# TensorE's instructions in the written order, in a hybrid mixer block on one Trainium2 core

## Chip, core and metric

The program runs on one core of a Trainium2 chip (trn2). What is compared is the device time of one execution in microseconds (us). Five engines work in parallel, each with an instruction stream of its own: TensorE (PE in the profile, its weight loads PEld), VectorE (DVE), ScalarE (ACT), GpSimd (POOL) and SyncE (SP, which here issues all DMAs). They wait for each other by semaphores.

## What is computed

One layer of a streaming encoder over 1024 tokens of 1024 channels. u is the RMS-normalised input; it is multiplied by one wide input matrix, and the product is split over four branches of 256 channels:

```python
u = rms_norm(h, norm_mix_pre[l])
z = u @ w_in[l]
(hq, hf, hi, hg, pz, sq, sk, sv, iq, ik, iw, mq) = jnp.split(z, split_pts, axis=-1)
y_a = hgrn2_mixer(hq, hf, hi, hg, lb_all[l], hgrn_norm[l])   # gated linear recurrence, 4 heads
y_b = pool_mixer(pz, pool_w[l], pool_scale[l])               # trailing means over 2, 4, 8, 16 tokens
y_c = dsa_mixer(sq, sk, sv, iq, ik, iw)                      # index scores, top 256 keys, attention
mk, mv = jnp.split(rms_norm(mem, norm_mem[l]) @ w_mem_kv[l], 2, axis=-1)
y_m = mem_attention(mq, mk, mv)                              # attention into 256 memory tokens
merged = None
for bi, y in enumerate((y_a, y_b, y_c, y_m)):
    term = jax.nn.sigmoid(u @ w_gate[l, bi]) * (y @ w_branch[l, bi])
    merged = term if merged is None else merged + term
h = h + rms_norm(merged @ w_out[l], norm_mix_post[l])
gt, up = jnp.split(rms_norm(h, norm_ffn_pre[l]) @ w_ffn_gate_up[l], 2, axis=-1)
h = h + rms_norm((jax.nn.silu(gt) * up) @ w_ffn_down[l], norm_ffn_post[l])
```

## The kernel before

The tokens are worked in two halves of 512 (`HT`), and the second half begins while the first one's FFN is still running. A float32 product is made of three products of the rounded type fp32r: every operand is split into a high and a low part (`split_ps`, `Unit.split`), and hi x hi, hi x lo and lo x hi are added up in a PSUM bank.

Two kinds of work make up the program. The dense stream is a list, `prog`, of units (`Unit`): the weights of a unit (128 x 1024 values) are loaded into `raw` by SP, split into `wh` by ScalarE (L265) and into `wl` by GpSimd or VectorE (L266), and multiplied by 24 matmuls. `raw`, `wh` and `wl` have three buffers each, so that a unit's split waits for the products of the unit three before it. A product is either channel-major (`fm_mm`, L284 to L286, 512 columns, two PSUM banks "B") or token-major (`tm_units`, L341 to L343, four banks "A" or two "B" and two "C"). The other kind is side work: index scores, top-k, the sparse attention (dsa), the memory attention, the HGRN recurrence, pooling, and the normalisation of u. Each of these is a Python generator that emits a few instructions for all engines and yields. The loop over the list sets the written order:

```python
advance(i - e.hold)
e.mm(e)
step_side()
if e.evac is not None:
    e.evac(e)
```

So one step of every running generator is written between a unit's products and the evacuation of its bank; `need(...)` writes all that is left of a generator at once. Side work takes its PSUM bank from the class that `side_tag` names at the time (`spt`).

The kernel is written for a tile framework whose scheduler takes this program, goes through it by priority (the earlier written, the higher) with a model of the engines, and decides for each engine the order of its instructions: where the next one of an engine isn't ready in that model, a later one that is goes ahead. It then sets the semaphores. On the chip each engine follows its fixed order.

Steps that the prediction speaks of, in written order:

- The start: `mem_front` loads the memory tokens and x and squares x; `uT_gen0` has then three kinds of steps: `rstd_cols` (L438, four matmuls with a vector of ones over `xsq`), `to_rows` (L443, the 1 / rms of each token as rows in PSUM), and the pairs of u tiles (L486, L155, L489). One step is written behind each of the four memory units (`kv_units`). Then come the unit `mq[0]`, `kv_out` (`mem_rstd` with L438 and L443 once more, then mk and mv with the transposes L464), the unit `mq[1]`, four units hg (`thg`), with `rows1` (L443) behind the second.
- The first half's middle: four units iq with the index scores behind them (`score_gen`, L596 and L597, relu on ScalarE, accumulation on VectorE), two units pz, four units hi (`thi`), two units sq. `pool_gen` makes the trailing means on VectorE (L952 to L972), splits them into `phl`, and multiplies by L978 to L980: for the first group behind the second hi unit, for the second group behind the third. HGRN of head 0 has L905 behind the first sq unit and L915, L916 behind the second.
- The second half's scores, four tiles with up to 1024 keys, are written behind its units iq and hi.
- `wout_units(1)` ends with tiles that come one after another; `u2_gen` transposes each normalised tile `un` (L203). The last step of it is written by `all_of(S["u2", 1])`, ahead of the FFN's first two units, which `by_token_halves` writes as four products of 24 matmuls over 256 tokens each, the first tokens of both units first.

Of the kernel before, what the change touches and what calls it, by code (L numbers as in the profile page):

```python
# [35 lines left out]
def tile_hybrid_block(ctx, tc, x, x_t, mem_t, cols, w_in, w_gate, w_branch, w_out, hgrn_norm,  # L36
# [3 lines left out]
    x, out = x[0], out[0]  # L40
# [22 lines left out]

    # ---------------------------------------------------------------- constants
    ident = st([128, 128], name="ident")
# [8 lines left out]
    def build_masks():  # L74
        """Inside a block of 32 steps: where s lies in the left and t in the right half of a block of 2^(l+1)."""
        for l in range(6):
            if l < 5:
                m = st([128, 128], name="mtmp", tag="t2")
                h = 1 << l
                nb = 64 // h  # L80
                nc.gpsimd.memset(m, 1.0)
                v = m.rearrange("p (n w) -> p n w", w=2 * h)
                nc.gpsimd.affine_select(out=v, in_=v, pattern=[[-2 * h, nb], [0, 2 * h]], compare_op=OP.is_ge,
                                        fill=0.0, base=0, channel_multiplier=1)
                nc.gpsimd.affine_select(out=v, in_=v, pattern=[[2 * h, nb], [0, 2 * h]], compare_op=OP.is_ge,
                                        fill=0.0, base=h - 1, channel_multiplier=-1)
                nc.gpsimd.memset(v[:, :, 0:h], 0.0)
            else:
                m = ident
            for r in range(4):  # L90
                rs = slice(32 * r, 32 * r + 32)
                nc.vector.tensor_copy(masks[rs, l, :], m[rs, rs])
# [23 lines left out]
    def load_small():  # L116
        dma(hgain, bcast_row(hgrn_norm, 256))
        # lower bound: cumsum over depth of softmax over depth, minus its first row
        lg = st([128, 8], name="lg")
        nc.vector.tensor_tensor(lg[:, 4:8], lb_in, lb_in, op=OP.subtract)  # L120
        nc.scalar.activation(lg[:, 0:4], lg[:, 4:8], AF.Exp)
        rc = st([128, 4], name="lrc")
        nc.vector.reciprocal(rc, lg[:, 0:4])
        nc.vector.tensor_tensor(lg[:, 4:8], lg[:, 0:4], rc, op=OP.mult)
        nc.vector.tensor_tensor(lbt[:, :, 0], lg[:, 4:8], lg[:, 4:8], op=OP.subtract)
        nc.vector.tensor_scalar(lbt[:, :, 1], lbt[:, :, 0], -1.0, 1.0, op0=OP.mult, op1=OP.add)
        pw = st([128, 256], name="pw", tag="t2")
        nc.gpsimd.memset(pw, 0.0)
        for g in range(4):
            r0 = 64 * (g % 2)  # L130
            c0 = (g // 2) * 128 + r0
            dma(pw[r0:r0 + 64, c0:c0 + 64], pool_w[0, g])
        hi = poolw[:, 0].rearrange("p a b -> p (a b)")
        lo = poolw[:, 1].rearrange("p a b -> p (a b)")
        nc.scalar.activation(hi, pw, AF.Copy)
        nc.gpsimd.tensor_tensor(lo, pw, f32(hi), op=OP.subtract)

    # ---------------------------------------------------------------- persistent data
    h1d = [dr.tile([128, D], F32, name=f"h1d{i}", tag=f"h1d{i}") for i in range(8)]
# [12 lines left out]

    # ---------------------------------------------------------------- small helpers
    def copy(o, i):
# [6 lines left out]
    def twice_silu(o, t, p):  # L161
        """2 p sigmoid(p), as p (1 + tanh(p / 2))."""
        nc.scalar.activation(t, p, AF.Tanh, scale=0.5)  # L163
        nc.vector.scalar_tensor_tensor(o, t, 1.0, p, op0=OP.add, op1=OP.mult)  # L164
# [11 lines left out]
    def mean_eps(ss):  # L176
        """Its part of mean + eps, of half of the columns."""
        ms = st([128, 1], name="mse", bufs=10)
        nc.vector.tensor_scalar(ms, ss, 1.0 / D, EPS, op0=OP.mult, op1=OP.add)
        return ms  # L180
# [24 lines left out]

    # ---------------------------------------------------------------- side work
    side = []
# [22 lines left out]

    # ---------------------------------------------------------------- main stream
    class Unit:
        """One step of the dense stream: weights of up to 1024 columns per partition, and a product."""

# [64 lines left out]
    def by_token_halves(u0, u1, x_of):  # L299
        """Two units as four products over half of the tokens each: the first tokens of both come first."""  # L300
        ev0, ev1 = u0.evac, u1.evac

        def mm0(u):
            u.p = pt("B")

        def mm1(u):
            u.p = pt("B")
            for n0 in (0, 256):
                for v in (u0, u1):
                    fm_mm(v, v.p, *x_of(), n0 + 256, n0=n0)  # L310

        u0.mm, u1.mm, u1.hold = mm0, mm1, 1
        u0.evac, u1.evac = None, lambda u: [ev0(u0), ev1(u1)]

    def tm_units(w, ktiles, k0, cols, xT_of, tags, evac, pre=None, defer=0, apart=0):
        """Token-major product: four token tiles accumulate over the k tiles, two per unit.
        The last `defer` units run tile by tile, so that the tiles end one after another;
        the first `apart` of them keep their weights outside of the ring."""
        acc, res, waiting = [], [], []
        n = sum(wd for _, wd in cols)  # L320
        nu = ktiles // 2
        for ui in range(nu):
# [29 lines left out]
            u = Unit(loads, (2, n), mm, end if ui == nu - 1 and not defer else None, pre=pre if ui == 0 else None)  # L352
# [38 lines left out]

    # ================================================================ memory tokens
    S = {}

    def mem_front(load):
        """Memory tokens with their gain; 1 / rms comes in after the product."""
        mh, ml = S["memT"] = (st([128, NK, 256], F32R, name="memh", tag="b8"),
# [35 lines left out]
    def rstd_cols(acc, tag):  # L433
        """1 / rms of every token, a column per token tile, out of the partial sums of squares."""
        n = acc.shape[-1] // 128
        p = pt(tag)
        for t in range(n):
            nc.tensor.matmul(p[:, t:t + 1], acc[:, t * 128:(t + 1) * 128], ones[:, 0:1], start=True, stop=True)  # L438
        return rstd_of(p[:, 0:n], D, n)
# [27 lines left out]

    # ================================================================ u of one half
    def load_x(i):
# [38 lines left out]
    def rows1():  # L508
        """1 / rms of the second half's tokens."""
        rs = st([128, 4], name="xrs")  # L510
        for t in range(4):
            xt = load_x(4 + t)
            r = rstd_of(square_sum(xt, xt), D)
            nc.vector.tensor_copy(rs[:, t:t + 1], r[:, 0:1])
        yield
        copy(rrow, to_rows(rs, 4, spt()))
# [9 lines left out]

    # ================================================================ DSA
    def ikd_alloc(h):
# [18 lines left out]
    def stack_evac(p):  # L547
        """Two heads of 64 channels as [hi; lo] and [lo; hi] over the partitions."""
        q = st([128, 2, HT], F32R, name="qst", tag="b4")
        lo = st([128, HT], F32R, name="qlo", tag="t2")  # L550
# [140 lines left out]

    # ================================================================ memory attention
    def ev_mq(h, c):
# [54 lines left out]

    # ================================================================ HGRN
    def ev_hg(h):  # L750
# [60 lines left out]
    def hgrn_gen(h, hd, fa, fb):  # L811
# [5 lines left out]
        for c in range(4):  # L817
            s = slice(c * 128, (c + 1) * 128)
# [4 lines left out]
        def levels(ls):  # L823
            """Both factors of the decayed products over the halves of every block of 2^(l+1) steps."""
            def views(i, l):
# [18 lines left out]
        def gram32(todo):  # L844
            """Products inside the blocks of 32 steps, of up to four levels in one bank."""
            p = spt()
# [19 lines left out]
        p = spt()  # L866
# [67 lines left out]

    # ================================================================ pooling
    def ev_pz(h, c):
# [48 lines left out]

    # ================================================================ gates, as 2 sigmoid(p) = 1 + tanh(p / 2)
    def gate_units(h, br, ykey, fs, first=False, last=False, pre=None):
# [29 lines left out]

    # ================================================================ output projection
    def stag(tag):
# [45 lines left out]

    # ================================================================ FFN
    def ffn_units(h, groups, late):
# [73 lines left out]

    # ================================================================ program
    def all_of(gen):
# [109 lines left out]
    prog += [lambda: all_of(S["u2", 1])] + ffn_units(1, (8, 8, 6), lambda: None)  # L1253
    run()

# [31 lines left out]
```

## Time and profile before

| | |
|---|---|
| median of 2 runs | 1835.7 us (1834.63 to 1836.76) |
| span of the profiled execution, first to last instruction | 1831.4 us |
| TensorE busy | 1758.4 us, 96% |
| VectorE busy | 1054.4 us, 58% |
| ScalarE busy | 722.3 us, 39% |
| GpSimd busy | 880.5 us, 48% |
| DMA queue of the kernel's loads, share of the 16 engines | 34.0% |
| mean granted TensorE clock | 0.986 |

The profile is that of one execution. Its span lies 4.3 us under the median of the runs, which have some time around the span. The times in the rows count from the span's start. An engine's idle time ahead of an instruction stands in brackets with the instruction that released it. Matmuls overlap in the records: the distance from one start to the next, not the duration of one, is what a product costs in a dense stretch. A product of two operands of plain float32 shows as two records.

### The profile page before, as it was taken

To read this page: it belongs to the slowest core of one execution; us is meant where nothing else is said; L and a number is where in the kernel's file an instruction comes from. 1 tells how busy PE (TensorE), PEld (TensorE's weight loads), DVE (VectorE), ACT (ScalarE), POOL (GpSimd) and SP (SyncE) were. 2 spreads that over 40 slices of the span, in tenths; PEclk is the share of its full clock that TensorE was granted. 3 is DMA by queue.
4 is the path that set the end of the run, shared out by engine and by line. 5 is a ranking of instruction groups with operands and counts; after the bars stand their busy time and mean duration, and the time that the engine had idled before them with its cause. 6 is when DMAs were issued, how large, how long until landed. Compare 5 with 4: busy or idle time off the path is not lost. (4 is left out here: it accounts for less than half of the span.)

```text
span 1831.4 us, 25977 instructions
## 1 busy us (share of the span) xinstructions
PE 1758.4 (96%) x10000; PEld 1462.8 (80%) x10000; DVE 1054.4 (58%) x1972; ACT 722.3 (39%) x1175; POOL 880.5 (48%) x567
## 2 busy tenths in 40 slices
PE   7988989999999999999999999989999999999998
PEld 6877778888887787878888877878878888888886
DVE  6577999482345999999982674567541411011114
ACT  5653435443435533333323454534433422322232
POOL 5533435566643244444444353346566555455453
PEclk9998999999999999999999999999999999999999
DMA  6523222343244232323222442223323543333332
GB/s 180 174 59 86 76 73 74 90 140 117 86 135 120 75 104 82 108 78 94 82 81 90 159 155 73 67 87 84 96 73 92 166 150 100 96 95 101 92 103 70
DMA packets 262300, 185.99 MB, mean 102 GB/s; under 512 B 15904, under 2 KB 234144, under 8 KB 262048
## 3 DMA queue, kind: packets, MB, share of 16 engines
q1 hardware_dynamic: 262176, 184.33, 34.0%
q8 instruction: 79, 1.29, 0.3%
q14 instruction: 45, 0.37, 0.1%
HBM read 169.62 MB, written 10.49 MB: 98 GB/s over the span
## 5 line engine op out<-in xcount | busy, mean ns | idle before, releaser
L266 POOL TENSOR_TENSOR wl<-raw,wh 128x1024 fp32r<-128x1024 f32 (+3 forms) x269 | 636.5, 2367 | 804.6 <-ACT wh L265 770.3
L265 ACT ACTIVATE wh<-raw 128x1024 fp32r<-128x1024 f32 (+4 forms) x274 | 278.3, 1018 | 659.0 <-issue 273.5
L284 PE MATMUL psB<-uTh,wh 128*128 128x512 f32 x816 | 327.2, 401 | 3.1 <-DVE hw L164 2.5
L285 PE MATMUL psB<-uTl,wh 128*128 128x512 f32 x816 | 321.4, 394 | 0.5 <-DVE uTl L489 0.3
L286 PE MATMUL psB<-uTh,wl 128*128 128x512 f32 x816 | 321.7, 394 | 0.0
L284 PE MATMUL psB<-u2h,wh 128*128 128x512 f32 (+1 forms) x720 | 278.4, 387 | 1.4 <-DVE qlo L554 0.9
L285 PE MATMUL psB<-u2l,wh 128*128 128x512 f32 (+1 forms) x720 | 277.2, 385 | 1.2 <-DVE u2l L159 1.2
L286 PE MATMUL psB<-u2h,wl 128*128 128x512 f32 (+1 forms) x720 | 276.8, 385 | 0.0
L284 PEld LDWEIGHTS psB<-uTh,wh 128*128 128x128 f32 x816 | 155.2, 190 | 35.9 <-DVE hw L164 2.9
L286 PEld LDWEIGHTS psB<-uTh,wl 128*128 128x128 f32 x816 | 154.9, 190 | 33.5
L285 PEld LDWEIGHTS psB<-uTl,wh 128*128 128x128 f32 x816 | 155.3, 190 | 32.5 <-DVE uTl L489 1.2
L619 DVE MAX8 m<-sc 128x8 f32<-128x384 f32 (+5 forms) x192 | 170.7, 891 | 3.7
L620 DVE MATCH_REPLACE8 sc<-m,sc 128x384 f32<-128x384 f32 (+5 forms) x192 | 168.0, 875 | 0.1
L284 PEld LDWEIGHTS psB<-u2h,wh 128*128 128x128 f32 x720 | 135.2, 188 | 28.3 <-PE psB L286 1.3
L285 PEld LDWEIGHTS psB<-u2l,wh 128*128 128x128 f32 x720 | 135.3, 188 | 27.8 <-DVE u2l L159 1.4
L286 PEld LDWEIGHTS psB<-u2h,wl 128*128 128x128 f32 x720 | 135.2, 188 | 27.2
L164 DVE SCALAR_TENSOR_TENSOR silu<-silu,psB 128x512 f32<-128x512 f32 x44 | 30.1, 683 | 203.5 <-ACT silu L163 203.4
L1085 DVE SCALAR_TENSOR_TENSOR silu<-silu,psB 128x512 f32<-128x512 f32 x44 | 30.1, 683 | 87.1 <-PE psB L286 87.1
L1003 DVE SCALAR_TENSOR_TENSOR sig<-sig,psC 128x512 f32<-128x512 f32 x48 | 32.9, 685 | 78.6 <-PE psC L286 70.3
L1006 POOL TENSOR_TENSOR merged<-merged,sig 128x512 f32<-128x512 f32 x48 | 64.5, 1345 | 16.1 <-DVE sig L1003 12.7
L341 PE MATMUL psA<-wh,hTh 128*128 128x512 f32 x176 | 69.2, 393 | 0.0
L342 PE MATMUL psA<-wl,hTh 128*128 128x512 f32 x176 | 68.6, 390 | 0.0
(383 smaller groups left out, 3060.2 us busy)
## 6 DMA issues: line engine op xcount, KB each, us to landing
raw<-in_w_ffn_gate_up_dram SPq DMA_DIRECT2D x88, 512.0 KB, 3.9
raw<-in_w_gate_dram SPq DMA_DIRECT2D x64, 512.0 KB, 3.9
raw<-in_w_ffn_down_dram SPq DMA_DIRECT2D x44, 512.0 KB, 3.7
raw<-in_w_in_dram SPq DMA_DIRECT2D x36, 512.0 KB, 4.1
praw<-in_w_branch_dram SPq DMA_DIRECT2D x64, 128.0 KB, 3.5
raw<-in_w_out_dram SPq DMA_DIRECT2D x16, 512.0 KB, 3.8
xt<-in_x_t_dram SPq DMA_DIRECT2D x12, 512.0 KB, 6.0
xt<-in_x_dram SPq DMA_DIRECT2D x12, 512.0 KB, 4.9
```

The source lines that it names most:

```text
L164: nc.vector.scalar_tensor_tensor(o, t, 1.0, p, op0=OP.add, op1=OP.mult)
L265: nc.scalar.activation(self.hi[:, r], self.raw[:, r], AF.Copy)
L266: eng.tensor_tensor(self.lo[:, r], self.raw[:, r], f32(self.hi[:, r]), op=OP.subtract)
L284: nc.tensor.matmul(p[:, ns], whi[:, k, :], xh[:, k, ns], start=(k == 0), stop=False)
L285: nc.tensor.matmul(p[:, ns], whi[:, k, :], xl[:, k, ns], start=False, stop=False)
L286: nc.tensor.matmul(p[:, ns], wlo[:, k, :], xh[:, k, ns], start=False, stop=(k == nk - 1))
L341: nc.tensor.matmul(acc[t][:, 0:n], xh[:, k, ts_], v.hi[:, a, :], start=(k == 0), stop=False)
L342: nc.tensor.matmul(acc[t][:, 0:n], xh[:, k, ts_], v.lo[:, a, :], start=False, stop=False)
L619: nc.vector.max(m8, sc)
L620: nc.vector.match_replace(sc, m8, sc, DROPPED)
L1003: nc.vector.scalar_tensor_tensor(o, sg, 1.0, u.q, op0=OP.add, op1=OP.mult)
L1006: nc.gpsimd.tensor_tensor(m, m, sg, op=OP.add)
```

## The change

The loop over the list is run inside a block that tells the scheduler to leave the order of TensorE as it is written. The scheduler still orders VectorE, ScalarE, GpSimd and SP by its model. No instruction is added, removed or altered; comments and docstrings are dropped without a change of the line numbers.

```diff
     prog += wout_units(1)
     prog += [lambda: all_of(S["u2", 1])] + ffn_units(1, (8, 8, 6), lambda: None)
-    run()
+    with tc.manual_schedule(engines={mybir.EngineType.PE}):
+        run()
```

## Rows read from the trace of the kernel before

**Rows 1.** The page's head and busy time: engine, busy us, share, instructions; clock by slice; a costly group.

```profile
span 1831.4 us, 25977 instructions
...
PE 1758.4 (96%) x10000; PEld 1462.8 (80%) x10000; DVE 1054.4 (58%) x1972; ACT 722.3 (39%) x1175; POOL 880.5 (48%) x567
...
PEclk9998999999999999999999999999999999999999
...
L266 POOL TENSOR_TENSOR wl<-raw,wh 128x1024 fp32r<-128x1024 f32 (+3 forms) x269 | 636.5, 2367 | 804.6 <-ACT wh L265 770.3
```

**Rows 2.** Sums by stretch: busy us and instructions by engine, granted clock, DMA share.

```profile
150.05:153.55 3.50, 3.50 (x25) 3.46 (x25) 3.43 (x7) 1.09 (x3) 1.58 (x1) 1.00 0.11 23
...
153.60:187.70 34.10, 25.63 (x113) 22.40 (x112) 29.24 (x65) 9.06 (x15) 10.12 (x4) 0.80 0.26 75
...
161.20:167.20 6.00, 5.99 (x21) 5.70 (x22) 4.58 (x10) 2.19 (x4) 2.42 (x1) 0.50 0.22 63
...
187.70:300.00 112.30, 104.32 (x710) 86.74 (x709) 107.16 (x280) 53.45 (x90) 45.98 (x29) 0.97 0.27 76
...
1080.10:1086.10 6.00, 6.00 (x26) 4.96 (x27) 2.77 (x2) 3.51 (x5) 5.76 (x3) 1.00 0.30 87
...
1480.00:1800.00 320.00, 320.00 (x1414) 264.96 (x1413) 34.38 (x50) 87.96 (x109) 167.62 (x80) 1.00 0.32 97
```

**Rows 3.** TensorE's timeline, the first 46 us: start, us, instruction, idle before.

```profile
6.34 0.58 PE L284 MATMUL psA<-memh,wh 128*128 128x256 f32 x1 [6.34 <-ACT wh L265]
...
12.57 0.41 PE L284 MATMUL psA<-memh,wh 128*128 128x256 f32 x1
...
23.47 1.50 PE L438 MATMUL psC<-ones,xsq 128*128 128x1 f32 x8 [2.26 <-DVE xsq L498]
...
26.74 2.08 PE L443 MATMUL psC<-ident,rstd 128*128 128x128 f32 x8 [0.93 <-POOL rstd L168]
...
45.83 0.38 PE L464 MATMUL psC<-ident,mvT 128*128 128x128 f32 x2
...
45.96 0.37 PE L341 MATMUL psA<-wh,uTh 128*128 128x264 f32 x1
```

**Rows 4.** VectorE's and GpSimd's timelines, the same stretch.

```profile
22.72 0.69 DVE L498 TENSOR_TENSOR xsq<-xsq 128x512 f32<-128x512 f32 x1
...
39.41 0.14 DVE L173 TENSOR_SCALAR ms<-psC 128x2 f32<-128x2 f32 x1
...
40.31 1.28 POOL L489 TENSOR_TENSOR uTl<-xt,uTh 128x512 fp32r<-128x512 f32 x1
```

**Rows 5.** TensorE's timeline, 157 to 188 us.

```profile
157.12 0.31 PE L341 MATMUL psA<-wh,uTh 128*128 128x320 f32 x1
...
161.21 0.79 PE L978 MATMUL psC<-phl,poolw 128*128 128x512 f32 x1 [3.78 <-ACT phl L155]
...
179.78 1.94 PE L905 MATMUL psA<-vg,hw 128*128 128x64 f32 x8 [4.69 <-DVE svt L772]
...
187.66 0.33 PE L915 MATMUL psA<-vg,att 128*128 128x64 f32 x2
```

**Rows 6.** VectorE's timeline at 180 us.

```profile
180.26 0.68 DVE L975 TENSOR_TENSOR phl<-pz,phl 128x512 fp32r<-128x512 f32 x1
```

**Rows 7.** TensorE's timeline, 1459 to 1467 us.

```profile
1459.11 0.48 PE L284 MATMUL psB<-u2h,wh 128*128 128x256 f32 x2
...
1466.44 1.07 PE L203 MATMUL psA<-ident,un 128*128 128x128 f32 x8 [0.68 <-DVE un L195]
```

**Rows 8.** TensorE's timeline at four single places.

```profile
242.80 0.65 PE L870 MATMUL psA<-hw 128*32 128x32 f32 x16 [5.59 <-DVE yc L159]
...
612.34 0.50 PE L596 MATMUL psC<-ikd,qst 128*128 128x512 f32 x1 [1.30 <-ACT relu L599]
...
1080.09 0.50 PE L284 MATMUL psB<-uTh,wh 128*128 128x512 f32 x1 [2.51 <-DVE hw L164]
...
1359.32 0.63 PE L931 MATMUL psA<-ident,hw 128*128 128x128 f32 x4 [1.03 <-DVE hw L924]
```
## Prediction

> **What bounds the kernel now.** Read the page first: TensorE is busy 1758.4 of 1831.4 us and holds its full clock in nearly every slice [rows 1]. From 1480 to 1800 us it has no idle time at all: 1414 products in 320 us, one each 0.226 us [rows 2]. So a microsecond in which TensorE stands idle is a microsecond of the kernel, unless it takes the place of one that TensorE stands already. Second, go through TensorE's timeline from start to end with the code beside it. The written order is: a unit's products, then one step of every side generator, then the unit's evacuation. Where an instruction of a side step stands behind products that the code has after it, the scheduler has moved it, and the count of those products is what the change will take out of that hole. Third, look at what ended the idle time ahead of the moved instruction: where the row names a releaser, its input really came late, and in the written order TensorE would have waited for it with nothing to do.
>
> The result of that reading: at most places of the 1831 us the order is already the written one. I find it changed at the start (up to 73 us), around the pooling branch of the first half (153 to 188), in the index scores of the second half (580 to 634), at the last token tile before the last FFN (1459), and at eight smaller places with 4 to 20 products each.
>
> **The start.** Today the scheduler runs all of the four memory products nearly back to back. In the code, step 1 of the generator of u (L438, the sums of squares) stands behind the first of them, the rows (L443) behind the second. The first one's 24 products run from 6.34 to 12.57, and xsq is ready at 22.72 + 0.69 = 23.41 [rows 3, 4]. In the written order TensorE stands from 12.6 to 23.4; L438 starts when it does today, but the other 72 memory products are still to come. The second 24 take 5 us at the low clock that follows a long wait (the first 24 took 6.2), so L443 starts near 30.0, not at 26.74: u is 3.3 us late. Today u's last part is ready at 40.31 + 1.28 = 41.6 [rows 4]; then 44.9, and the first mq unit ends at 45.3. Behind it the code has kv_out, a chain through VectorE, GpSimd, ScalarE and back (ms, rstd, L443, mk, mvT, L464). Today that took from 39.41 to 45.83 beside the products of the second mq unit [rows 3, 4]; then nothing is beside it: 6 us, and after it that unit, 24 x 0.226 = 5.4. That is 56.7 where today it is 45.96: 10.7 us late. The clock may fall once more during kv_out (3 us), and the rows of the second half (L443 in rows1) may come late for their written place (up to 5). I take 13, between 10 and 19.
>
> **Pooling, first half.** The matmuls of the first pooling group (L978) stand behind the second of the four hi units, those of the second group behind the third. Today 25 products of later units run first, at 0.14 us each (25 in 3.5) [rows 2], and TensorE still waits 3.78 for phl, until 161.21; the second group's wait is hidden behind a whole hi unit, a whole sq unit and six more products, until its phl is ready at 180.26 + 0.68 = 180.9 [rows 5, 6]. VectorE sets both times: busy 29.24 of the 34.1 us, most of it top-k and pooling in turn [rows 2]. Written order: wait from 153.6 to 161.2; the group until 163.9; the third hi unit, partly at the low clock, until 169; wait until 180; the group until 182; the fourth hi unit at the low clock, 6.4; two sq units of 5.5 and L905 with about 1.5. That is 200.9 for L915, today at 187.66 [rows 5]: 13 us. VectorE has less to give way to when TensorE, and so GpSimd's weight splits, stand still; I take 11, between 7 and 14.
>
> **The last token tile.** all_of(u2) puts the transposes of the fourth tile ahead of the whole FFN. Its un is ready at 1466.4; today 40 products of the first two FFN units run from 1459.11 on, ahead of it [rows 7]. Written order: TensorE stands 7.3 us. The 40 products have 256 columns; at half of 0.226 they are worth 4.5, and the hole less the 0.68 that is idle today is 6.6. After such a wait the clock is low, about 3 us more. I take 8, between 4.5 and 9.
>
> **The scores, 580 to 634.** A step emits up to eight pairs of L596 and L597 through two psC buffers; each needs ScalarE's relu and VectorE's accumulation to free the next. Today 40 products in all lie between the pairs, and in three of the blocks TensorE waits over a microsecond beside, as at 612.34 [rows 8]. Worth at most 27 x 0.14 + 13 x 0.226 = 6.7; the pairs can come a little sooner when nothing stands between them. I take 5, between 1 and 7.
>
> **The smaller places.** An upper end is the moved products by 0.226: 10 at the second half's pooling (2.3) and 12 at L931 (2.7); 4, 6, 7, 5 and some 20 short ones at the others (in all 5). I take 9, between 5 and 13; the 13 has one more fall of the clock, at L931, whose wait grows from 1.03 to 4 [rows 8].
>
> **What comes back.** VectorE is the busiest engine from 187.7 to 300: 107.16 of 112.3 us [rows 2], and TensorE is idle for 8.0 there (104.32 busy), 5.59 of it at 242.80, for VectorE [rows 8]. It isn't idle while TensorE stands between 153 and 188: top-k goes on and ends sooner. I take 4 back, between 0 and 9.
>
> **The weights.** Nothing else is moved: the instructions of TensorE issue no DMA. But a unit's split waits for the products three units before it (wh has three buffers), and SP's load of raw waits for the split, so ScalarE, GpSimd and SP stand still too when TensorE does. Their cover is three units, some 16 us, and starts again with TensorE; I cost this at nothing, and a unit whose weights come late after a long wait would cost some 2.4, GpSimd's part of its split [rows 1].
>
> **The clock.** Six microseconds after the 3.78 us wait all ran at 0.50 of full speed, 1.2 GHz; after the 2.51 us wait at 1080 the clock stayed at 1.00 [rows 2, 8]. So I charge a fall to long waits alone: 3 us each, half of six. The Trainium skill speaks against this change here: "TensorE: Matmul & The Clock Gate", section "HAM oscillation — how this bites in real kernels", tells that waits between groups of matmuls put the array back to half clock, so that each group starts cold and pays again. The first row agrees, the second is a wait that it didn't follow. By the page the new waits at kv_out, L931 and in the scores would each cost a fall, and the sum would be some 10 us higher; that is a rival below.
>
> **The sum.** 13 + 11 + 8 + 5 + 9 - 4 = 42. The profiled execution's span is 1831.4 us, and the median of the runs is 1835.7, so 4.3 lie around the span. 1831.4 + 42 + 4.3 = 1877.7; I say 1878 us, 2.3% slower. From the ends of all parts: 1835.7 + 18.5 = 1854 and 1835.7 + 62 = 1898.
>
> **Rivals.** (1) VectorE gets ahead, and the kernel is not measurably slower. Place: 153 to 300 us. Each microsecond that TensorE stands goes to a saturated VectorE, so the second phl comes 4 us sooner, and the 8.0 us of waits up to 300 go with the fall of the clock behind the longest (3). It decides when top-k is over before the scores of its last tile are used. Price: 42 less 4, less the 7 not yet counted, less 4 where the score pairs flow freely: 27, so 1863. For it: VectorE is the only engine near 100% there. Against it: it does its work in a fixed order, and top-k instructions stand between those for which TensorE waits.
> (2) The clock falls after every new wait: three more falls, 10 us, 1888. For it the row at 161, against it the one at 1080.
> (3) The other engines are ordered anew around a TensorE that stands still: top-k instructions go in front of evacuations, and from 640 to 900, where VectorE is as full as it is from 187.7 on, TensorE waits at places where it doesn't now. One more wait like 5.59 in each of the five dsa tiles or so is 28 us: 1905. Against it: where the order is the written one already, the scheduler has no reason to do so.
> (4) The change does nothing, because order and waits stay as they are: 1836. Against it: the timeline shows orders that the code doesn't have.
>
> **How the numbers follow.** Chances: the forecast 0.38, with 1866 to 1890 as its own range; rival 1 0.27; rival 2 0.18; rival 3 0.11; rival 4 0.06. Two per cent, about what a measurement can tell from no change, end at 1872.4. Three quarters of the forecast (0.29) and rivals 2 and 3 lie above: 0.58. The rest of the forecast, rivals 1 and 4 within: 0.40. Faster needs the waits of today to go and no new ones to come: 0.02. The range of 8 in 10 goes from 1856, below rival 1, to 1900, between rivals 2 and 3.
>
> **What would show it.** In the new profile: no product of a memory unit between 12.6 and 23.4; the clock low after that; L978 at 161 and about 180 (plus the 13 of the start) with waits of 7 and 11 us ahead of them; a wait of 7 us ahead of L203 before the last FFN; TensorE's idle time up by some 35 us with the same 10000 instructions. The wait at 242.80 tells rival 1 from the forecast, the clock behind kv_out and L931 rival 2, waits between 640 and 900 rival 3. I am wrong if the late inputs come sooner once TensorE stands for them, above all xsq and phl.

## The result and the profile after

The changed kernel takes 1882.8 us in the median (1881.27 to 1884.27), 1.026 times the kernel before, with an interval of 1.023 to 1.029: 2.6% slower. The forecast was 1878, between 1856 and 1900. Two executions among those of the experiments below, of 6810.5 and 2000.2 us, ran at a low granted clock (0.461 and 0.827) and are in none of the times.

The page of the changed kernel answers to [rows 1]: span, busy time by engine, granted clock by slice.

```profile
span 1879.5 us, 25981 instructions
...
PE 1767.8 (94%) x10000; PEld 1471.0 (78%) x10000; DVE 1049.2 (56%) x1972; ACT 726.2 (39%) x1177; POOL 877.1 (47%) x567
...
PEclk8898999999999999999999999999999999999999
```

The same 10000 instructions of TensorE. Idle time is span less busy time: 1831.4 - 1758.4 = 73.0 before, 1879.5 - 1767.8 = 111.7 after, so 38.7 more. The other 9.4 of the 48.1 is busy time: the same products at a lower clock (the mean granted clock is 0.974, before 0.986).

TensorE waits for these in the changed kernel (what waited, what it waited for, us in total, times, longest us). Ahead of the same instructions the kernel before waits 2.26 (L438), 3.78 (the first L978 alone), and 0.68 (L203) [rows 3, 5, 7].

```profile
PE psC L978 <- ACT phl L155: 14.7, 2, 7.4
PE psC L438 <- DVE xsq L498: 10.7, 1, 10.7
PE psC L596 <- ACT relu L599: 8.0, 11, 1.3
PE psA L203 <- DVE un L195: 7.8, 2, 7.0
```

TensorE's timeline at the start, against [rows 3]:

```profile
7.43 0.58 PE L284 MATMUL psA<-memh,wh 128*128 128x256 f32 x1 [7.43 <-ACT wh L265]
...
13.39 0.41 PE L286 MATMUL psA<-memh,wl 128*128 128x256 f32 x1
...
24.54 1.84 PE L438 MATMUL psC<-ones,xsq 128*128 128x1 f32 x8 [10.73 <-DVE xsq L498]
...
49.10 1.22 PE L443 MATMUL psC<-ident,rstd 128*128 128x128 f32 x4 [1.04 <-POOL rstd L168]
52.92 1.09 PE L464 MATMUL psC<-ident,mvT 128*128 128x128 f32 x4 [2.60 <-DVE mvT L461]
53.66 0.78 PE L284 MATMUL psB<-uTh,wh 128*128 128x512 f32 x1
...
61.43 0.28 PE L341 MATMUL psA<-wh,uTh 128*128 128x264 f32 x1
...
73.42 1.65 PE L443 MATMUL psC<-ident,xrs 128*128 128x128 f32 x6 [4.74 <-ACT P L725]
```

VectorE's timeline says why L438 and L464 start when they do, against [rows 4]:

```profile
23.70 0.69 DVE L498 TENSOR_TENSOR xsq<-xsq 128x512 f32<-128x512 f32 x1
...
52.36 0.75 DVE L461 TENSOR_TENSOR mvT<-psA,mrstd 128x256 f32<-128x256 f32 x2
```

No product stands between 13.8 and 24.5; xsq, which needs nothing from TensorE, ends at 24.39, one us later than before, as the first product of this execution does. What is lost is the 72 products that stood in front of L438 before. The second mq unit starts behind L464, and L341 comes 15.5 us later than before (45.96).

TensorE's timeline at the first half's pooling, against [rows 5, 6]:

```profile
182.29 0.79 PE L978 MATMUL psC<-phl,poolw 128*128 128x512 f32 x1 [7.37 <-ACT phl L155]
...
197.12 0.80 PE L978 MATMUL psC<-phl,poolw 128*128 128x512 f32 x1 [7.29 <-ACT phl L155]
...
209.42 1.00 PE L905 MATMUL psA<-vg,hw 128*128 128x64 f32 x8
...
215.80 0.33 PE L915 MATMUL psA<-vg,att 128*128 128x64 f32 x2
```

At four other places, against [rows 7, 8]:

```profile
267.10 0.43 PE L870 MATMUL psA<-hw 128*32 128x32 f32 x8 [4.56 <-DVE yc L159]
...
642.94 0.79 PE L596 MATMUL psC<-ikd,qst 128*128 128x512 f32 x1 [1.28 <-ACT relu L599]
...
1396.19 0.86 PE L931 MATMUL psA<-ident,hw 128*128 128x128 f32 x4 [3.83 <-DVE hw L924]
...
1507.57 1.73 PE L203 MATMUL psA<-ident,un 128*128 128x128 f32 x7 [7.04 <-DVE un L195]
```

And sums by stretch (columns as in [rows 2]), of the changed kernel:

```profile
182.24:197.07 14.83, 7.12 (x27) 6.16 (x27) 14.22 (x33) 2.32 (x3) 2.34 (x1) 0.73 0.12 35
...
208.80:324.70 115.90, 110.78 (x745) 92.61 (x744) 108.86 (x280) 55.83 (x93) 48.25 (x30) 0.99 0.30 83
...
597.65:706.50 108.85, 97.87 (x429) 77.37 (x428) 86.95 (x144) 50.18 (x94) 27.98 (x14) 0.94 0.27 76
...
1396.20:1399.60 3.40, 3.40 (x11) 2.81 (x12) 0.69 (x1) 0.60 (x1) 0.00 (x0) 0.53 0.00 0
...
1507.50:1512.50 5.00, 4.93 (x23) 4.96 (x24) 1.38 (x2) 1.19 (x2) 0.00 (x0) 0.50 0.98 341
```

and two of the kernel before, the time from the end of the first phl's high part (for which L978 waits) to that of the second's, as in the first line above, and the same 429 instructions at the scores:

```profile
161.16:180.05 18.89, 14.15 (x58) 12.36 (x58) 17.11 (x33) 5.65 (x10) 7.70 (x3) 0.77 0.28 82
...
569.30:666.70 97.40, 91.52 (x429) 74.41 (x428) 81.75 (x133) 49.97 (x94) 28.05 (x14) 0.98 0.31 84
```

The second phl's high part ends there at 180.04:

```profile
179.41 0.63 ACT L155 ACTIVATE phl<-pz 128x512 fp32r<-128x512 f32 x1 [4.75 <-DVE pz L972]
```

Read the two lines of the scores (597.65 to 706.50 and 569.30 to 666.70) together: 11.5 us more, of which 10.98 - 5.88 = 5.1 is idle time and 97.87 - 91.52 = 6.35 is busy time, with the clock at 0.94 against 0.98. The waits of about 1 us at L596 cost less than the low clock among them.

**Where the 48 us arise.** The dense stream has 6912 products in every kernel here (L284 to L286, L341 to L343; where the start is mended, 24 of them stand in a function of their own), in one order but for some products near a moved step. The table takes the n-th of them, says when it starts in the kernel before, and how much later the n-th starts in the others, in us of their profiled executions. The columns behind "whole" belong to the experiments below.

| n, before | whole | start | first half | scores | rest | start mended | pooling | tail | banks | all | all, free | pooling, free |
|---|---|---|---|---|---|---|---|---|---|---|---|---|
| 144, 46.0 | 15.5 | 13.8 | -0.8 | 0.4 | 0.4 | 3.8 | 14.4 | 14.1 | 13.6 | 4.7 | -0.9 | -0.5 |
| 312, 92.9 | 21.8 | 21.9 | -0.8 | 0.5 | 0.7 | 12.3 | 20.6 | 20.3 | 19.9 | 10.1 | -4.0 | -0.4 |
| 400, 124.6 | 21.1 | 21.8 | 2.9 | 0.5 | -0.9 | 13.1 | 19.9 | 19.6 | 19.2 | 16.4 | 0.6 | -0.6 |
| 700, 213.8 | 28.2 | 21.6 | 10.7 | 0.5 | -0.9 | 20.1 | 20.1 | 26.8 | 26.3 | 16.2 | -2.7 | -1.8 |
| 850, 266.8 | 24.7 | 22.1 | 7.3 | 1.6 | 0.6 | 18.2 | 19.2 | 23.3 | 22.8 | 13.2 | -3.3 | -1.9 |
| 2050, 569.3 | 28.4 | 22.1 | 10.2 | 2.4 | 1.3 | 21.5 | 23.2 | 27.3 | 26.5 | 17.1 | -2.6 | -1.8 |
| 2350, 666.7 | 39.8 | 20.6 | 8.7 | 13.0 | -0.1 | 32.0 | 32.2 | 38.1 | 32.4 | 20.5 | -4.4 | -3.2 |
| 3100, 864.3 | 37.4 | 22.1 | 10.2 | 10.5 | -0.2 | 29.5 | 29.7 | 35.6 | 31.6 | 18.3 | -3.3 | -1.6 |
| 4150, 1163.1 | 35.8 | 22.4 | 10.3 | 10.1 | -0.2 | 29.5 | 29.7 | 34.0 | 32.3 | 17.1 | -4.5 | -1.5 |
| 4450, 1250.0 | 36.9 | 22.5 | 10.4 | 10.1 | 1.1 | 31.3 | 22.9 | 35.4 | 34.1 | 10.4 | -11.2 | -8.2 |
| 4900, 1368.9 | 41.2 | 22.6 | 12.7 | 12.3 | 5.4 | 36.1 | 28.6 | 39.6 | 38.9 | 16.0 | -11.0 | -8.0 |
| 5350, 1471.1 | 48.0 | 22.5 | 12.6 | 12.3 | 12.3 | 43.0 | 34.4 | 40.3 | 45.9 | 16.7 | -11.0 | -8.0 |

### The profile page after: what moved, and what is told of

Same layout as the page of the kernel before. It is cut to its first block, busy times and chain, and to the rows that moved or that the text cites. A ratio compares the mean times of both kernels' runs of the same rounds, so it can differ in the third digit from the quotient of the medians.

```text
span 1879.5 us, 25981 instructions
## 1 busy us (share of the span) xinstructions
PE 1767.8 (94%) x10000; PEld 1471.0 (78%) x10000; DVE 1049.2 (56%) x1972; ACT 726.2 (39%) x1177; POOL 877.1 (47%) x567
## 5 line engine op out<-in xcount | busy, mean ns | idle before, releaser
L284 PE MATMUL psB<-uTh,wh 128*128 128x512 f32 x816 | 328.7, 403 | 3.6 <-DVE hw L164 2.5
L286 PE MATMUL psB<-uTh,wl 128*128 128x512 f32 x816 | 322.0, 395 | 0.0
L284 PE MATMUL psB<-u2h,wh 128*128 128x512 f32 (+1 forms) x720 | 279.4, 388 | 1.3 <-DVE qlo L554 0.8
L286 PE MATMUL psB<-u2h,wl 128*128 128x512 f32 (+1 forms) x720 | 277.6, 386 | 0.0
L284 PEld LDWEIGHTS psB<-uTh,wh 128*128 128x128 f32 x816 | 156.3, 191 | 37.0 <-DVE hw L164 2.9
L286 PEld LDWEIGHTS psB<-uTh,wl 128*128 128x128 f32 x816 | 155.6, 191 | 33.9
L284 PEld LDWEIGHTS psB<-u2h,wh 128*128 128x128 f32 x720 | 136.1, 189 | 28.3 <-PE psB L286 1.2
L286 PEld LDWEIGHTS psB<-u2h,wl 128*128 128x128 f32 x720 | 135.9, 189 | 27.3
L1006 POOL TENSOR_TENSOR merged<-merged,sig 128x512 f32<-128x512 f32 x48 | 64.7, 1347 | 11.7 <-DVE sig L1003 7.9
L341 PE MATMUL psA<-wh,hTh 128*128 128x512 f32 x176 | 69.3, 394 | 0.0
L343 PE MATMUL psA<-wh,hTl 128*128 128x512 f32 x176 | 68.6, 390 | 0.0
```

Source lines behind the costliest of these rows:

```text
L284: nc.tensor.matmul(p[:, ns], whi[:, k, :], xh[:, k, ns], start=(k == 0), stop=False)
L286: nc.tensor.matmul(p[:, ns], wlo[:, k, :], xh[:, k, ns], start=False, stop=(k == nk - 1))
L341: nc.tensor.matmul(acc[t][:, 0:n], xh[:, k, ts_], v.hi[:, a, :], start=(k == 0), stop=False)
L343: nc.tensor.matmul(acc[t][:, 0:n], xl[:, k, ts_], v.hi[:, a, :], start=False, stop=e)
L1006: nc.gpsimd.tensor_tensor(m, m, sg, op=OP.add)
```

## The experiments

Times of all, each with the kernel before on the same chip:

| kernel | median us | before | ratio (95%) |
|---|---|---|---|
| written order at the start alone | 1854.6 | 1832.3 | 1.012 (1.008 to 1.016) |
| in the first half alone | 1843.1 | 1832.3 | 1.006 (1.004 to 1.008) |
| at the second half's scores alone | 1843.9; 1844.1 | 1832.3; 1834.6 | 1.007 (1.004 to 1.009); 1.005 (1.002 to 1.007) |
| in the rest alone | 1846.2 | 1832.3 | 1.008 (1.005 to 1.010) |
| whole, start mended | 1875.8 | 1833.0 | 1.023 (1.022 to 1.025) |
| whole, pooling mended | 1868.7 | 1833.0 | 1.019 (1.018 to 1.021) |
| whole, last tile mended | 1876.2 | 1833.0 | 1.023 (1.022 to 1.025) |
| whole, four banks at the scores | 1880.2 | 1833.0 | 1.026 (1.025 to 1.028) |
| whole, all mended | 1850.7 | 1831.8 | 1.010 (1.008 to 1.011) |
| all mended, scheduler orders TensorE | 1820.6 | 1831.8 | 0.994 (0.992 to 0.995) |
| pooling mended, scheduler orders TensorE | 1826.8 | 1831.8 | 0.997 (0.996 to 0.998) |

**The written order in one stretch at a time.** Theory 1: each place costs its own waits, and the places add up. Theory 2: the other engines, ordered anew, make them depend on each other. Two functions enter and leave the block and stand in the list of units:

```diff
+    def on():
+        held.append(tc.manual_schedule(engines={mybir.EngineType.PE}))
+        held[-1].__enter__()
+
+    def off():
+        held.pop().__exit__(None, None, None)
...
-    with tc.manual_schedule(engines={mybir.EngineType.PE}):
-        run()
+    run()
...
-    prog += [front1] + thg(1)
+    prog += [on, front1] + thg(1)
```

The start, up to skik:

> TensorE keeps the written order only from the first memory unit to the unit skik of the first half (up to 120 us); behind that the scheduler orders it as before. Theory 1 (each place costs its own waits, and the places add up): the 20.7 us that the changed kernel is later at the last hg product than the kernel before, so about 1835.7 + 20.7 = 1856, with waits of 10.7 ahead of the first L438, 2.6 ahead of L464 and 4.7 ahead of L443 of rows1. Theory 2 (the places depend on each other, since the other engines are ordered anew through the whole program, or the late start is given back where VectorE is the bound, 187 to 300 us): clearly less than 20 or more than 25, and the sum of the four kernels of this group is not the 47 of the whole change.

Measured 22.3 us in the medians, 21.9 at product 312 and the same up to the end: the start's cost arises there and nothing of it is given back later, not even from 187 to 300 us, where VectorE is the bound.

The first half:

> TensorE keeps the written order only from head(0, 0) to the first half's last gate unit (120 to 540 us), the pooling of the first half among it. Theory 1: the changed kernel is 6 to 7 us later at the end of this stretch than at its start (5.3 of it at pooling, 2.9 at L631, 2 given back at L870), so about 1842; waits of 7 us ahead of both L978. Theory 2: when TensorE isn't late already, VectorE is no further ahead, and pooling costs the 11 that was forecast, so 1847 or more.

10.8 us in the medians. The waits ahead of the two L978 are 7.37 and 7.29, the same as in the whole to a hundredth, and pooling costs 7.8 (products 400 to 700) against 7.1, so a late start gives VectorE no lead there; theory 2's reason falls. The time is nearer to 1842 than to 1847. What is beyond theory 1 is 3.7 between 93 and 125 us, which the whole doesn't have, and 2.3 from a wait at L870 (below).

The scores:

> TensorE keeps the written order only from thg(1) to the two sq units of the second half (540 to 680 us): u2's transposes and the index scores with their two psC buffers. Theory 1: 12.3 us, the part of the changed kernel in that stretch (11.5 at the scores), so about 1848; three falls of the clock between 600 and 680. Theory 2 (the scores are only dear because the rest runs in the written order too): the 5 that was forecast, so about 1841.

11.6 us in the medians. To see the places, the same kernel ran once more, with a sharper question:

> The kernel with the written order only from thg(1) to the two sq units of the second half once more, for a profile at the usual clock. Theory 1 (TensorE's stand at the scores lets VectorE get ahead with top-k, and some of it is given back at the attention tiles of 745 to 865 us): 11 to 12 us later than the kernel before at the last sq product, 2 to 2.5 given back until 865, and at the end 9 to 10, so about 1842. Theory 2 (the 2.5 that the changed kernel gives back there comes from its late start): 11 to 12 at both points and at the end, about 1844.

Its line for the scores, and one of its waits:

```profile
571.65:679.70 108.05, 97.34 (x429) 77.09 (x428) 87.03 (x144) 50.22 (x94) 27.98 (x14) 0.95 0.27 76
```

```profile
PE psA L870 <- DVE hw L841: 2.9, 1, 2.9
```

The scores cost 13.0 - 2.4 = 10.6 with no other part of the change, and 2.5 comes back until product 3100: theory 1 of both. So VectorE does get ahead while TensorE stands there, and the waits for P (L676) shrink. The end is at 12.3 all the same, because of a wait of 2.9 for hw ahead of L870 at 1343 us, where TensorE's order is the scheduler's; only this kernel and the one before it in the table have it. It isn't a new order: TensorE and VectorE go there in the order of the kernel before. One instruction of VectorE, the last L840 ahead of the L841 that makes hw, took 2.57 us where it took 0.41 before, beside one of GpSimd's weight splits that had begun just ahead of it (the last section shows such a pair once more). This kernel:

```profile
1339.11 2.57 DVE L840 TENSOR_TENSOR hw<-hw 128x256 f32<-128x256 f32 x1
```

```profile
1339.03 2.37 POOL L266 TENSOR_TENSOR wl<-raw,wh 128x1024 fp32r<-128x1024 f32 x1 [2.92 <-ACT wh L265]
```

and the kernel before, where that split starts at 1328.99, lasts 3.08 and leaves VectorE's instruction alone:

```profile
1329.08 0.41 DVE L840 TENSOR_TENSOR hw<-hw 128x256 f32<-128x256 f32 x1
```

Counted from VectorE's instruction before, the two splits start within a few hundredths of a microsecond of the same moment. So a small shift in time decides here, not an order.

The rest:

> TensorE keeps the written order only from the FFN of the first half to the end (680 to 1831 us). Theory 1: 8.2 us as in the changed kernel (last token tile 6.8, L931 4.4, three places of 1.1 to 1.5, and 2.5 and 4.4 given back at 640 to 900 and 1158), so about 1844. Theory 2 (the gains of this stretch come from TensorE being late and not from its order): without the 6.9 given back, about 1851.

13.9 us in the medians, 12.3 in the profile: theory 2, nearly. L931 (4.3) and the last tile (6.9) cost what they cost in the whole, but from 667 to 864 us nothing is won (-0.1), and until 1163 nothing either.

The four ends make 22.5 + 12.6 + 12.3 + 12.3 = 59.7, the whole 48.0. So the places don't simply add up. Of the 11.7, 4.6 is the wait at L870 twice, which is none of a place's cost, and the rest lies in pieces between 93 and 267 us (6.4) and between 667 and 1163 (4.4), less 5.2 at the scores, where three of the four kernels run 1.4 to 1.5 faster than the kernel before with the same order. Which fall of the clock comes or goes in each of them I didn't follow.

**The start mended.** L438 behind the third memory unit, L443 inside the fourth, the memory tokens' chain behind mq[0], L464 behind mq[1], and the rows of the second half three steps later (four yields in place of one):

```diff
-    prog += kv_units + [lambda: need(S["u0"])]
+    prog += kv_units[0:3] + [lambda: next(S["u0gen"]), kv_units[3], lambda: all_of(S["u0gen"])]
...
-    prog += [mq[0], kv_out, mq[1]] + [lambda: start(rows1())]
+    prog += [mem_rstd, mq[0], kv_out, mq[1], mv_rows] + [lambda: start(rows1())]
```

> The whole program stays in the written order, but the start is written anew: L438 behind the third memory unit, L443 behind 7 of the 24 products of the fourth, the memory tokens' L438 ahead of mq[0], their L443 behind mq[0], the transposes L464 behind mq[1], the rows of the second half four steps later. Theory 1 (the place in the code costs the time, since nothing is written beside the chains of the start): TensorE at L631 near 95 comes back to 75 to 78, 17 to 20 us less, so about 1864; no wait over 3 us before 70. Theory 2 (the inputs come late for any order): L438 still starts at 24 and u is ready no sooner, so at most 8 us are won and the result is 1875 or more.

Only 5 us: 1.0261 - 1.0231 = 0.3% in the ratios, whose intervals overlap, and 5.0 in the profiles. TensorE's timeline of this kernel; its lines stand 3 to 7 lower, L740 is L733, L446 is L443, L495 is L489:

```profile
38.55 0.50 PE L285 MATMUL psB<-uTl,wh 128*128 128x512 f32 x1 [2.44 <-POOL uTl L495]
...
62.57 1.71 PE L740 MATMUL psC<-ident,P 128*128 128x128 f32 x8 [2.39 <-ACT P L732]
...
86.52 1.13 PE L446 MATMUL psA<-ident,xrs 128*128 128x128 f32 x8 [2.72 <-DVE mmx L729]
```

The time is theory 2's, the mechanism neither's: the chains of u, mk and mv were mended as theory 1 says (3.8 late at product 144, where the whole is 15.5 late), and then 8.5 is lost again until product 312, at the memory attention's P (the clock is at 0.62 from 62.5 to 68) and at the rows of the second half. Moving the rows three steps later put them behind VectorE again: the row names mmx, which stands right behind a read of PSUM bank A.

**Pooling mended.**

```diff
-        yield
+        for _ in range((3 + 2 * c) if h == 0 else 2):
+            yield
         p = spt()
         nc.tensor.matmul(p, poolw[:, 0, c, :], hl[:, 0, :], start=True, stop=False)
```

> The whole program stays in the written order, but each pooling group of the first half has its matmuls two (first group) and four (second group) steps later, those of the second half one step later. Theory 1 (TensorE waits 7.4 and 7.3 for phl only because nothing else is written ahead of L978): both waits go, and 5 to 9 us are won, so 1874 to 1878. Theory 2 (VectorE, with GpSimd's splits beside it again, sets the pace of this stretch): the wait comes back at the next input from VectorE (svt ahead of L905, or yc ahead of L870, 4.7 and 5.6 in the kernel before), and less than 3 us are won.

12 us won, more than either theory. In the first half theory 2 holds in good part: both waits of 7 go, and this one comes:

```profile
197.53 1.30 PE L905 MATMUL psA<-vg,hw 128*128 128x64 f32 x5 [9.04 <-DVE svt L772]
```

Products 400 to 850 lose -0.7 where the whole loses 3.6: 14.7 us of waits are worth 4.3. The large gain is in the second half, which neither theory counted: there one step later takes away the wait for phl and the low clock behind it, -6.8 (products 4150 to 4450) against +1.1, and the kernel is faster there than the kernel before.

**The last tile mended.**

```diff
             for n0 in (0, 256):
+                if n0:
+                    all_of(S["u2", 1])
                 for v in (u0, u1):
...
-    prog += [lambda: all_of(S["u2", 1])] + ffn_units(1, (8, 8, 6), lambda: None)
+    prog += [lambda: next(S["u2", 1])] + ffn_units(1, (8, 8, 6), lambda: None)
```

> The whole program stays in the written order, but the last token tile's transposes (L203) are written behind the 48 products of the first 256 tokens of the FFN's first two units. Theory 1: the 7.0 us wait shrinks to under 2, as 48 products of 256 columns cover some 5.4, and 5 to 8 us are won (the fall of the clock at 1502 goes too), so about 1876. Theory 2 (the products ahead of it only push the evacuation chain later): 2 us or less.

Theory 1: 5 us in the ratios, though their intervals overlap; the place shows it clearly: products 4900 to 5350 lose 0.7 in place of 6.8. What is left of the waits at this place:

```profile
1502.46 0.39 PE L285 MATMUL psB<-u2l,wh 128*128 128x256 f32 x1 [1.66 <-DVE u2l L159]
...
1506.75 1.03 PE L203 MATMUL psA<-ident,un 128*128 128x128 f32 x8
```

**Four banks at the scores.**

```diff
-                    p = spt()
+                    p = pt("CB"[a]) if h == 1 and side_tag[0] == "C" else spt()
```

> The whole program stays in the written order, but while the second half's hi units run the score pairs take psC and psB buffers in turn, four in place of two. Theory 1 (the two psC buffers make L596 wait): the 8.0 us that L596 waits for relu in psC fall to under 3, the falls of the clock between 642 and 673 go, 5 to 8 us are won, so about 1876. Theory 2 (the three tiles that relu writes and VectorE's accumulation, 0.75 a pair, set the pace): TensorE runs at most two pairs further ahead, waits at the end of each block instead, and the result is within 2 us of 1883.

Theory 2's time (1.0263 against 1.0261), but not its mechanism. This kernel's waits at L596, and its stretch with the same products as the two lines of the scores above:

```profile
PE psB L596 <- ACT relu L599: 4.9, 3, 1.6
...
PE psC L596 <- ACT relu L599: 0.3, 1, 0.3
```

```profile
595.80:699.10 103.30, 94.50 (x430) 76.56 (x430) 83.89 (x138) 49.69 (x94) 28.04 (x14) 0.95 0.29 80
```

Eleven waits become four, and the scores cost 5.9 in place of 11.5. Until 1163 the whole gets back 4.0, this kernel 0.1, and the profiled execution ends 2.4 us sooner than the whole. The medians show none of it. So the two psC buffers make about half of the cost; three waits of 1.6 stay, released by ScalarE's relu. Whether the three relu tiles or VectorE hold it back there wasn't separated.

**All mended, in the written order and by the scheduler.** To the three edits above come smaller ones (the rows two steps later instead of three, memory attention and L905 one step later), and the second half's scores in portions of two pairs, half of them in the middle of a unit's products:

```diff
+                    if t == 2:
+                        step_scores()
                     ts_ = slice(t * 128, (t + 1) * 128)
...
+                if h == 1 and o + 512 < L:
+                    yield
             if c == 3:
                 nc.vector.memset(sc[0:64, L - 64:L], NEG)
```

> The whole program in the written order, all mended places at once: the start (with the rows of the second half two steps later instead of four, and the memory attention one step later), pooling, L905 of the first head one step later, the last token tile, L931 one step later, and the second half's score pairs in portions of two pairs per generator, half of them written in the middle of a unit's products. Theory 1 (the places add up): against the changed kernel 12 less at pooling, 5 at the last tile, 5 to 8 at the start, 4 at L931, 8 to 10 at the scores, in all 34 to 39, so 1842 to 1847 where the kernel before is at 1833. Theory 2 (what is won at one place comes back as a wait for VectorE at the next): 1855 or more. Neither gives a kernel faster than before.

> The same program text as the run with all mended places, but the scheduler orders TensorE too. Theory 1 (the scheduler goes by its model of what is ready, the text gives it only the priority): it undoes and redoes the order by itself, so within 5 us of the kernel before, 1828 to 1838, with second half's pooling 7 us better. Theory 2 (the text decides the order even so): the same as with the written order, 1842 to 1847.

In the written order 30 us are won against the changed kernel (1.0261 - 1.0097), between the two theories. The scores cost 3.4 in place of 11.5, and the clock stays at 1.00:

```profile
586.40:687.20 100.80, 92.26 (x430) 72.30 (x430) 84.95 (x145) 50.26 (x94) 28.22 (x14) 1.00 0.30 82
```

Of the 16.7 that are left, 16.4 are there at product 400 already: the start isn't mended, the rows still wait 4.0 for P, and L931 still costs 5.6: it stands behind the same product as in the whole, so my step didn't move it. The same text, with TensorE's order left to the scheduler, is at 0.6 at product 400 and ends 11 us ahead of the kernel before: 0.65% faster (0.5 to 0.8), theory 1, and better than it said; this version beats both kernels. The gap between the two, 1850.7 and 1820.6, is the price of the written order on the best text that I found, 1.7%.

**Pooling mended, by the scheduler.** The edit of the pooling matmuls in the kernel before:

> The kernel before (the scheduler orders TensorE), with nothing changed but the later steps of the pooling matmuls (two and four steps in the first half, one in the second). Theory 1 (the scheduler keeps what is written later behind; the run with mended pooling had no wait at the second half's L978, where the kernel before has 3.9 us and a low clock behind it): 6 to 8 us less than before, about 1826. Theory 2 (the scheduler moves L978 up again to the place where it stands today, or VectorE sets the pace and the wait goes elsewhere): within 2 us of 1833.

5 us won (0.3%, 0.2 to 0.4), a little under theory 1. One line of the kernel before and one of this, the same 186 instructions around the second half's L978:

```profile
1204.50:1250.00 45.50, 41.58 (x186) 34.08 (x185) 28.23 (x43) 19.86 (x29) 24.16 (x15) 0.92 0.31 90
```

```profile
1203.00:1241.80 38.80, 38.80 (x186) 32.38 (x185) 28.85 (x47) 19.56 (x29) 23.22 (x14) 1.00 0.35 106
```

45.50 - 41.58 = 3.92 us of idle time and 41.58 - 38.80 = 2.78 of slow products go. In the kernel before the scheduler had put L978 ahead of products that could have covered its wait; that its model had phl ready sooner than the chip is argued, not shown.

## Why the prediction was right

The mechanism was right: at the places that were named TensorE stood where a step's input came late. The sum was 42 and 48.1 was measured, but three of its terms lay outside of their own bounds. The start and the scores came out 14 us dearer, pooling, the last tile and the smaller places 10 cheaper; that the total is only 6 off is in part luck. By the table's column "whole":

| term | forecast (bounds) | measured | from |
|---|---|---|---|
| start | 13 (10 to 19) | 20.7 | 21.8 at product 312, less 1.1 that the first product is late |
| pooling | 11 (7 to 14) | 7.1 | products 400 to 700 |
| given back by 300 us | -4 (0 to -9) | -3.5 | 700 to 850 |
| scores | 5 (1 to 7) | 11.5 | 2050 to 2350 |
| last token tile | 8 (4.5 to 9) | 6.8 | 4900 to 5350 |
| smaller places | 9 (5 to 13) | 4.3 | the rest: -0.7, 3.6, -4.0, 1.1, 4.3 |
| first product | not in it | 1.1 | 7.43 against 6.34; it starts between 6.3 and 7.4 in the executions here, so this isn't the change |

**The start** was right in its mechanism and too small. L438 stood behind the first unit and waited from 13.8 to 24.5, as forecast; the 10.7 that I reckoned for the second mq unit were 14.4 (15.5 less 1.1), since that unit ran at the low clock (53.66 to 61.43, 7.8 in place of 5.4) and the first one met four waits for u's tiles (1.11, 0.62, 0.49 and 0.86). The two costs that I only let into the range, one more fall of the clock and 5 for the rows, both came. The clock stood at 0.50 from 48.2 to 58.4 and from 72.1 to 78.9: in a chain with nothing beside it the waits and the slow products behind them come together.

**Pooling**: the first wait was 7.37, as reckoned (7), the second 7.29 and not 11. The second phl came 14.8 us after the first instead of 18.9, so L915 came 7 late, not 13. For phl the prediction's own sign of being wrong came true: the late input came sooner once TensorE stood for it. The prediction saw the reason, that VectorE has less to give way to when the splits stand still, and took too little for it; GpSimd was busy for 2.34 in that stretch, before for 7.70. This is the step "VectorE gets ahead" of rival 1, at its place and with its 4 us, but within the forecast's bounds. The rest of rival 1 didn't come: the wait at L870, which was to tell the two apart, shrank from 5.59 to 4.56 only, and what came back later (3.5) was the forecast's 4.

**The scores** were the term that lay furthest outside of its bounds, 4.5 above them. The prediction priced the lost cover (40 products) and found 5 of idle time, which was right: 5.1. It charged a fall of the clock to long waits alone. The scores have none over 1.3 us, and the clock fell three times between 642 and 673 (the last three lines below). This cost is the step of the term that was wrong: the clock falls among short waits too. That is rival 2, at a place where it allowed one fall of 3 and the cost was 6.35. It holds at L931 too (0.53 behind a wait of 3.83), but not everywhere. From the sums by stretch of the changed kernel, behind a wait of 2.73, behind one of 2.53, and three times among the score pairs:

```profile
141.50:144.90 3.40, 3.40 (x15) 2.79 (x16) 3.40 (x11) 2.44 (x6) 0.20 (x1) 1.00 0.14 38
...
403.10:406.50 3.40, 3.40 (x9) 2.75 (x10) 3.40 (x5) 0.90 (x2) 1.58 (x1) 0.51 0.89 287
...
642.10:648.90 6.80, 5.59 (x19) 5.20 (x20) 6.16 (x13) 2.02 (x5) 0.00 (x0) 0.50 0.26 78
...
655.60:659.00 3.40, 3.14 (x11) 2.50 (x12) 3.17 (x6) 1.72 (x4) 0.00 (x0) 0.52 0.49 146
...
669.40:672.80 3.40, 3.40 (x9) 2.84 (x10) 3.40 (x7) 0.98 (x2) 0.00 (x0) 0.50 0.00 1
```

So rival 2 is half right: all that low clock added is 9.4, the falls that the forecast had counted among it, and not 10 on top of them. The Trainium skill's page "TensorE: Matmul & The Clock Gate" (section "HAM oscillation — how this bites in real kernels") tells of long waits between groups of matmuls, each group then starting at half clock; the waits of 3.83 and 7.04 here agree (0.53 and 0.50 behind them), and the scores, where the clock fell among waits of 1.3 at most, are a case that this section doesn't describe.

**The rest.** L931 cost 4.3, between its 2.7 and the 5.7 with one more fall. The last tile was a wait of 7.04, as read from un (7.3). No unit of the dense stream waited over a microsecond for its splits behind a long wait: the cover held. Rival 3 (waits of 28 us from 640 to 900) didn't come: that stretch gave 2.4 back; the one new wait for VectorE in a stretch left to the scheduler, 2.9 at L870 in two partial kernels, came without a new order. The "smaller places" fell short by this give-back and by 1.6 until 1163.

The interval of the ratio, 1878 to 1889, excludes the times of rivals 1 (1863), 3 (1905) and 4 (1836). Rival 2's 1888 lies in it, as the forecast does at its edge; between these two the terms decide, and they say: some of each.

## What to carry to other kernels

Where an engine's order is taken from the text, every step that is written behind one unit has to find its input ready there; read the chains of inputs first, place the consumer behind as many products as the chain lasts, and split a burst of side work into portions between products. A long wait that is hidden in this way brings back less than its length where another engine is full (14.7 us of waits at the first pooling, 4.3 won), and more than its length where the clock falls behind it (3.9 at the second pooling, 6.7 won). A scheduler's order can be improved by the text as well: find the waits it left, and write the waiting step one unit later.

## What the runs showed of the hardware

Short waits in a row can cost more clock than one long one: among the score pairs, with waits of 0.2 to 1.3 us, the clock stood at 0.50 to 0.52 for three stretches of 6.8, 3.4 and 3.4 us, and the slow products cost 6.35 us beside 5.1 of added idle time; behind the one wait of 3.83 it stood at 0.53 for 3.4 us.

An instruction of VectorE on 64x16 elements took 0.17 us or 2.28, by what GpSimd did beside it. From VectorE's and GpSimd's timelines of the kernel before:

```profile
170.40 2.28 DVE L967 TENSOR_TENSOR zhead<-pa,invc 64x16 f32<-64x16 f32 x1
```

```profile
169.72 2.94 POOL L266 TENSOR_TENSOR wl<-raw,wh 128x1024 fp32r<-128x1024 f32 x1 [5.11 <-ACT wh L265]
```

Both end at 172.7. In the changed kernel GpSimd is idle at that point and the same instruction takes:

```profile
190.22 0.17 DVE L967 TENSOR_TENSOR zhead<-pa,invc 64x16 f32<-64x16 f32 x1
```

The Trainium skill's page "SBUF — State Buffer" (section "SBUF: two separate sides") says that the two engines share a pair of ports as an exclusive lock for a whole instruction, for VectorE where an instruction has two inputs in SBUF, as this one has; the three rows agree, and so do the rows at L840 above. It makes VectorE faster while TensorE waits and the splits wait with it: of the 4.1 us by which the second phl came sooner, 2.8 lie in three such instructions (L967, L968 and, the other way, L969), and 1.2 in two waits of VectorE for TensorE and ScalarE.
